# S5 output products issued in pairs of state groups, and a stacked 64-token arm for experts with 129 to 192 tokens

## The chip, the cores and the metric

The kernel runs on one core of one Trainium2 chip, written for the core's own engines: TensorE (PE in the profile, with PEld for its weight loads), VectorE (DVE), ScalarE (ACT), GpSimd (POOL) and SyncE (SP, which issues most loads). The metric is the time of one execution on the device in microseconds (us), lower is better.

## The reference

The reference runs two blocks of two layers each on 512 tokens of width 1024, all in float32. The change lies in the second layer of the first block: an S5 mixer, and a mixture of experts (MoE).

```python
# S5: 64 groups of 16 channels with 64 complex states each, chunks of 64 tokens
bu = jnp.einsum('gpc,btgc->btgp', b_bar, u_c)            # input into the states
...
hs = hs + a_pow[None] * h[:, None]                       # states, carried from chunk to chunk
y = jnp.einsum('gcp,btgp->btgc', c, hs).real             # states to outputs
...
# MoE: each token goes to the 2 of 8 experts with the largest router logits
logits = xt @ w_router + b_router
top_v, top_i = lax.top_k(logits, 2)
gates = softmax(top_v)
y = sum_e gate[:, e] * ((silu(xt @ w1[e]) * (xt @ w3[e])) @ w2[e])    # 1024 -> 1408 -> 1024
```

The inputs are fixed by a seed. Computed from them by the reference's own formulas, the experts get 104, 105, 94, 110, 126, 176, 170 and 139 tokens: three of the eight have more than 128, and all three lie between 129 and 192.

## The kernel before

**Products in three parts.** Large matrices are split into a high part (`hi`, L76, a ScalarE copy to the type fp32r) and a low part (`lo`, L79, VectorE: source minus high part). A product is then three fp32r products, summed in one PSUM bank: high by high, high by low, low by high (`mm3`, L113 to 115, and `mm3s`, L120 to 122, where the weights are the moving operand of 512 columns and 128 tokens stand still in TensorE).

**S5.** The work goes through four batches B of 16 state groups. `front(B)` brings the inputs into U, forms the chunks' input sums (pS, L1018) and on VectorE the states at the start of each 8-token piece (Hs, real and imaginary part; L784 to 789 and the scan L1026, with the table Tab). `back(B)` then forms the outputs in two halves of four pairs q of state groups. For each group m of a pair it issues three plain float32 products on a quarter or half of the array: U by Tt (L1045, 128 rows, 64 columns at column 64m), and Hs[0] by Ca and Hs[1] by Ca (L1048, 64 rows and 64 columns at row and column 64m), all into the half bank p[64m:64m+64]. ScalarE takes the bank out (L1051), it is transposed (pYt, L1057), and VectorE and ScalarE finish it. While back(B) is on TensorE, projections of the next batch, the next front and the following GLU's products (pglu) are issued around it. A load of a batch's tables is queued on SP (L971 ff., L981).

**MoE.** The eight experts are taken one after the other (e = 0 to 7) in an order that the kernel sets from their counts; the three with two blocks come at e = 1, 4 and 7, where the trace has their products; `expert(e, blocks, ...)` is compiled for one block of 128 tokens, `(0,)`, and for two, `(0, 1)`, and a branch on the expert's count, read on each engine (L1607), chooses:

```python
with tc.If(n_e > 128) as two:
    expert(e, (0, 1), XG[e % 2], main, start, nxt, first, then, extra)
with two.Else():
    expert(e, (0,), XG[e % 2], main, start, nxt, first, then, extra)
```

In an expert, tokens are gathered by indirect DMA (`fetch`) and transposed into xg, high and low part (`turn`: pxg, L1456). Six chunks cc of the hidden width follow, 512 columns (256 of w1 and 256 of w3) in five and 256 in the sixth: for each of 8 k and each block, `mm3s` into ph; then silu (L1505, ScalarE), the product with the w3 half (hb, L1507, VectorE), and in `flush` the transposition of hb (phT, L1475) with its split into hT. At last come 11 k with two banks py of 512 columns, and copies of py to y (L1538 on ScalarE, L1539 on VectorE), which a DMA stores. The last expert keeps its output on chip: py is split into high and low parts (`own_y`) for the combining products pyo (L1640). The weights for the first four k of an expert's chunk 0 (`pre`) are split ahead of it, in the expert before; the others come through a ring of loaded units, each split by ScalarE and VectorE when its turn comes.

Of the kernel before, what the change touches and what calls it, by code (L numbers as in the profile page):

```python
# [21 lines left out]
D = 1024  # L22
# [26 lines left out]
class Core:  # L49
# [905 lines left out]
    def s5(self):  # L955
# [3 lines left out]
        with ExitStack() as ctx:  # L959
# [75 lines left out]
            def back(B, U, Hs):  # L1035
                Yn = b2.tile([128, 8, 8, 16], FT, tag="Yn", name="Yn", bufs=1)
                for hf in range(2):
                    Tt, Ca = load_out(B, hf)
                    p = self.bank("bk", "pY")
                    for qq in range(4):  # L1040
                        q = 4 * hf + qq
                        for m in range(2):
                            o = p[64 * m:64 * m + 64, 128 * qq:128 * qq + 128]
                            ks = slice(64 * m, 64 * m + 64)
                            mm(o, U[:, q, m], Tt[:, 2 * qq + m], start=True, stop=False,  # L1045
                               tile_position=(0, 64 * m))
                            for i in range(2):
                                mm(o, Hs[i][ks, q, 0:64],  # L1048
                                   Ca[ks, i, qq, 1:9].rearrange("p t c -> p (t c)"),
                                   start=False, stop=(i == 1), tile_position=(64 * m, 64 * m))  # L1050
# [124 lines left out]
    def _moe(self, m1, m2):  # L1175
# [271 lines left out]
                xs.append(x)  # L1447
            return xs

        def turn(xs, xt, b0=0):  # L1450
            for b, x in enumerate(xs, b0):
                for hf in range(2):
                    p = self.bank("pc", "pxg")
                    for k in range(4):
                        kk = 4 * hf + k
                        nc.tensor.transpose(p[:, k * 128:(k + 1) * 128], x[:, kk * 128:(kk + 1) * 128], ident)  # L1456
                    ks = slice(4 * hf, 4 * hf + 4)
                    q = p.rearrange("p (k n) -> p k n", n=128)
                    self.hi(xt[:, 0, ks, b], q)
                    self.lo(xt[:, 1, ks, b], q, xt[:, 0, ks, b])  # L1460

        def expert(e, blocks, xt, weights, start=None, nxt=None, first=(), then=None, extra=None):
# [3 lines left out]
            hT = {b: [m1.tile([128, 11, 128], FR, tag=f"hT{t}{b % 2}", name="hT") for t in "hl"] for b in blocks}  # L1466
            hb = {}

            def flush(cc, tag="pp"):
                nk = 2 if cc < 5 else 1  # L1470
                p = self.bank(tag, "phT")
                for bi, b in enumerate(blocks):
                    for j in range(nk):
                        c = (bi * nk + j) * 128
                        nc.tensor.transpose(p[:, c:c + 128], hb[cc, b][:, j * 128:(j + 1) * 128], ident)  # L1475
                for bi, b in enumerate(blocks):
                    q = p[:, bi * nk * 128:(bi + 1) * nk * 128]
                    th, tl = (t[:, 2 * cc:2 * cc + nk].rearrange("p k n -> p (k n)") for t in hT[b])
                    self.hi(th, q)
                    self.lo(tl, q, th)  # L1480

            for cc in range(6):
                n = 512 if cc < 5 else 256
                if extra and cc == 0:
                    extra()
                    got = start()
                ps = {b: self.bank("pc", "ph") for b in blocks}

                def product(w, u, b):
                    for k in range(4):  # L1490
                        kk = 4 * u + k
                        self.mm3s(ps[b][:, :n], xt[:, 0, kk, b % 2], xt[:, 1, kk, b % 2], w[0][:, k],
                                  w[1][:, k], start=(kk == 0), stop=(kk == 7))

                for u in range(2):
                    ahead = first and cc == u == 0
                    w = first if ahead else weights.take(pin=bool(mine) and cc == 1, fine=bool(first) and cc == 0)
                    for b in blocks:
                        if ahead and b and mine:
                            turn(mine, xt, 1)  # L1500
                        product(w, u, b)
                h2 = n // 2
                for b in blocks:
                    s = m2.tile([128, 256], FT, tag="sl", name="sl")
                    nc.scalar.activation(s[:, :h2], ps[b][:, :h2], AF.Silu)  # L1505
                    hb[cc, b] = m2.tile([128, 256], FT, tag="hb", name="hb", bufs=4)
                    v.tensor_tensor(hb[cc, b][:, :h2], s[:, :h2], ps[b][:, h2:n], op=OP.mult)  # L1507
                if cc:
                    flush(cc - 1)
            py = {}  # L1510
# [2 lines left out]
            for u in range(6):  # L1513
                w = weights.take(late=u == 5 and then is not None)
                for k in range(2 if u < 5 else 1):
                    kk = 2 * u + k
                    for b in blocks:
                        for j in range(2):
# [10 lines left out]
            for b in blocks:  # L1529
                if e == NE - 1 and not over:  # L1530
                    yh, yl = own_y(b)
                    for j in range(2):
                        c = slice(512 * j, 512 * j + 512)
                        self.hi(yh[:, c], py[b][j])
                        self.lo(yl[:, c], py[b][j], yh[:, c])
                    continue
                y = m2.tile([128, D], FT, tag="y", name="y")
                nc.scalar.activation(y[:, :512], py[b][0], AF.Copy)  # L1538
                v.tensor_copy(y[:, 512:], py[b][1])  # L1539
                if over:  # L1540
                    nc.scalar.dma_start(self.yo_d[128 * (b - 2):128 * (b - 1), :], y)
                else:
                    o = 128 * place(e, b)
                    nc.scalar.dma_start(self.y_d[o:o + 128, :], y)

        def own_y(b):

# [25 lines left out]
        for e in range(NE):  # L1573
# [36 lines left out]
                    which(k)  # L1610
            at, known = main.taken, dict(regs)
            extra = (lists, gates, None)[min(e, 2)]
            with tc.If(n_e > 128) as two:
                expert(e, (0, 1), XG[e % 2], main, start, nxt, first, then, extra)
            main.taken = at
            regs.clear()
            regs.update(known)
            with two.Else():
                expert(e, (0,), XG[e % 2], main, start, nxt, first, then, extra)
            regs.clear()  # L1620
            regs.update(known)

# [664 lines left out]
```

## Time and profile before

| what | value |
|---|---|
| time, median of 3 runs | 2566.69 us (2561.83 to 2568.28) |
| the profiled execution's own time | 2555.23 us |
| its span, first to last instruction | 2553.5 us |
| mean granted TensorE clock, share of full speed | 0.966 |
| TensorE busy | 2397.8 us, 94% of the span |
| VectorE busy | 1692.6 us, 66% |
| ScalarE busy | 1184.1 us, 46% |
| GpSimd busy | 489.7 us, 19% |
| DMA, mean over the span | 147 GB/s |

The busy times overlap, since the engines work side by side. TensorE's is summed over its whole span, and its matmuls run into each other like links of a chain: the time from one row's start to the next row's start says how long a product holds up the next, and the length in the row is longer than that. A row of the form "a<-b,c" writes tile a from tiles b and c, and 128x512 is its size, partitions by elements; on a TensorE row 64*64 or 128*128 is the part of the array (rows by columns) that it uses. In brackets stands the idle time before the row, and what ended it; "issue" means that no tile and no DMA did.

### The profile page before, as it was taken

The page shows a single profiled execution, that of the slowest core. Times are in us where ns is not written, and L with a number is a line of the kernel's source. Part 1 is how long each engine was busy: PE and PEld are TensorE (multiplying, and loading weights), DVE is VectorE, ACT ScalarE, POOL GpSimd, SP SyncE. Part 2 cuts the span into 40 slices and gives each one's busy share as a digit, 9 for nine tenths or more (in the row PEclk, how much of TensorE's full clock was granted, in tenths as well). Part 3 has the DMA queues.
Part 4 walks back from the last instruction along what each step waited for, and adds up shares of the span by engine and source line. Part 5 has one row for each costly group of instructions (what it writes and reads, how often), then busy time and mean ns, then how long its engine had stood idle before and what let it go on. Part 6 is the DMA issues. An engine that isn't in the chain of part 4 may idle for free. (4 is left out here: it accounts for less than half of the span.)

```text
span 2553.5 us, 35019 instructions
## 1 busy us (share of the span) xinstructions
PE 2397.8 (94%) x12769; PEld 1954.3 (77%) x12769; DVE 1692.6 (66%) x3554; ACT 1184.1 (46%) x2133; POOL 489.7 (19%) x585
## 2 busy tenths in 40 slices
PE   8999998979999999988988989999999998999997
PEld 7899987867788867766866777878776778787676
DVE  5877758868845663366567567666787557578466
ACT  5545434322433323245466456545656444556453
POOL 1010123676666101031000000110002013001103
PEclk9999999989999999979999999999999999999998
DMA  4323223556645552356578568834122222223111
GB/s 160 111 78 95 62 83 120 204 164 236 241 144 208 176 146 75 109 178 258 202 259 320 196 231 335 317 108 138 56 89 88 79 91 87 84 75 108 58 50 67
DMA packets 107744, 375.80 MB, mean 147 GB/s; under 512 B 23202, under 2 KB 49218, under 8 KB 77576
## 3 DMA queue, kind: packets, MB, share of 16 engines
q1 hardware_dynamic: 73440, 285.86, 32.4%
q0 software_dynamic: 13552, 61.18, 7.0%
q10 hardware_dynamic: 20536, 26.01, 2.9%
q8 instruction: 120, 1.97, 0.3%
q14 instruction: 96, 0.79, 0.1%
HBM read 335.76 MB, written 37.24 MB: 146 GB/s over the span
## 5 line engine op out<-in xcount | busy, mean ns | idle before, releaser
L79 DVE TENSOR_TENSOR wl<-raw,wh 128x1024 fp32r<-128x1024 f32 (+4 forms) x248 | 295.4, 1194 | 209.7 <-ACT wh L76 205.4
L79 DVE TENSOR_TENSOR wl<-ring,wh 128x1024 fp32r<-128x1024 f32 (+1 forms) x280 | 299.3, 1099 | 116.2 <-ACT wh L76 111.8
L76 ACT ACTIVATE wh<-raw 128x1024 fp32r<-128x1024 f32 (+5 forms) x262 | 246.0, 947 | 275.9 <-PE pp L114 85.8
L113 PE MATMUL pp<-xh,wh 128*128 128x512 f32 (+1 forms) x944 | 348.8, 375 | 4.4 <-ACT wh L76 1.1
L114 PE MATMUL pp<-xl,wh 128*128 128x512 f32 (+1 forms) x944 | 349.2, 370 | 3.2 <-DVE xl L79 3.1
L115 PE MATMUL pp<-xh,wl 128*128 128x512 f32 (+1 forms) x944 | 346.8, 369 | 0.0
L76 ACT ACTIVATE wh<-ring 128x1024 fp32r<-128x1024 f32 (+1 forms) x280 | 257.3, 956 | 123.4 <-PE ph L122 76.0
L113 PEld LDWEIGHTS pp<-xh,wh 128*128 128x128 f32 x944 | 179.9, 193 | 38.2 <-issue 3.7
L114 PEld LDWEIGHTS pp<-xl,wh 128*128 128x128 f32 x944 | 181.4, 192 | 32.0 <-DVE xl L79 4.0
L115 PEld LDWEIGHTS pp<-xh,wl 128*128 128x128 f32 x944 | 181.1, 192 | 28.2 <-issue 1.8
L121 PE MATMUL ph<-wl,xg 128*128 128x512 f32 (+1 forms) x484 | 181.5, 376 | 1.1 <-DVE wl L79 1.1
L122 PE MATMUL ph<-wh,xg 128*128 128x512 f32 (+1 forms) x484 | 180.6, 375 | 0.0
L120 PE MATMUL ph<-wh,xg 128*128 128x512 f32 (+1 forms) x484 | 179.3, 381 | 0.1
L115 PE MATMUL pf<-xh,wl 128*128 128x512 f32 (+1 forms) x384 | 145.4, 379 | 3.9 <-DVE wl L79 3.9
L114 PE MATMUL pf<-xl,wh 128*128 128x512 f32 (+1 forms) x384 | 145.8, 381 | 0.0
L113 PE MATMUL pf<-xh,wh 128*128 128x512 f32 (+1 forms) x384 | 145.3, 380 | 0.5 <-ACT xh L76 0.5
L121 PEld LDWEIGHTS ph<-wl,xg 128*128 128x128 f32 x484 | 91.2, 188 | 20.6 <-DVE wl L79 2.9
L122 PEld LDWEIGHTS ph<-wh,xg 128*128 128x128 f32 x484 | 91.0, 188 | 17.7
L1739 DVE SCALAR_TENSOR_TENSOR adaacc<-adaraw,sc,adaacc 128x512 f32<-128x512 f32 x84 | 92.5, 1101 | 17.9 <-DMA adaraw<-w_ada 16.8
L120 PEld LDWEIGHTS ph<-wh,xg 128*128 128x128 f32 x484 | 89.7, 189 | 16.8 <-ACT wh L76 0.6
L121 PE MATMUL py<-wl,hT 128*128 128x512 f32 x242 | 97.7, 404 | 4.1 <-DVE wl L79 4.1
L122 PE MATMUL py<-wh,hT 128*128 128x512 f32 x242 | 95.6, 397 | 0.0
(707 smaller groups left out, 5509.6 us busy)
## 6 DMA issues: line engine op xcount, KB each, us to landing
ring<-moe SPq DMA_DIRECT2D x120, 1024.0 KB, 6.2
raw<-w_in SPq DMA_DIRECT2D x30, 1024.0 KB, 4.9
adaraw<-w_ada POOLq DMA_DIRECT2D x24, 1024.0 KB, 5.4
raw<-w SPq DMA_DIRECT2D x22, 1024.0 KB, 5.7
ring<-moe SPq DMA_DIRECT2D x24, 512.0 KB, 5.5
raw<-w SPq DMA_DIRECT2D x16, 704.0 KB, 4.2
raw<-w_glu SPq DMA_DIRECT2D x8, 1024.0 KB, 5.1
raw<-w_out SPq DMA_DIRECT2D x8, 1024.0 KB, 4.8
```

Source lines behind the costliest of these rows:

```text
L76: return self.nc.scalar.activation(dst, src, AF.Copy, **kw)
L79: return (eng or self.nc.vector).tensor_tensor(dst, src, hi.bitcast(FT), op=OP.subtract)
L113: mm(ps, wh, xh, start=start, stop=False)
L114: mm(ps, wh, xl, start=False, stop=False)
L115: return mm(ps, wl, xh, start=False, stop=stop)
L120: mm(ps, ah, wh, start=start, stop=False)
L121: mm(ps, ah, wl, start=False, stop=False)
L122: return mm(ps, al, wh, start=False, stop=stop)
L1739: v.scalar_tensor_tensor(acc, r[:, k], s, acc, op0=OP.mult, op1=OP.add)
```

## The change

There are two parts, which don't touch each other.

In the S5 `back`, the products of the two groups m of a pair are taken in turn: both U by Tt products first, then both products with Hs[0], then both with Hs[1]. Number, sizes and places of the products stay as they were.

In the MoE, an expert with more than 128 tokens gets one of two arms: with more than 192, the two full blocks as before; with 129 to 192, an arm in which the second block has 64 tokens. Their high parts stand in columns 0 to 63 of one tile and the low parts in columns 64 to 127, so that for each k one product of 128 columns by the weights' high part forms high by high in PSUM rows 0 to 63 and low by high in rows 64 to 127, and one of 64 columns by the weights' low part adds high by low to rows 0 to 63 (`stacked`). `fold` adds the two halves of the bank: a ScalarE copy of rows 64 to 127 to SBUF and a VectorE addition. It is done once for each chunk ahead of silu and twice for each py.

```diff
@@ s5, back @@
+o = [p[64 * m:64 * m + 64, 128 * qq:128 * qq + 128] for m in range(2)]
 for m in range(2):
-    o = p[64 * m:64 * m + 64, 128 * qq:128 * qq + 128]
-    ks = slice(64 * m, 64 * m + 64)
-    mm(o, U[:, q, m], Tt[:, 2 * qq + m], start=True, stop=False, tile_position=(0, 64 * m))
-    for i in range(2):
-        mm(o, Hs[i][ks, q, 0:64], Ca[ks, i, qq, 1:9]..., start=False, stop=(i == 1), tile_position=(64 * m, 64 * m))
+    mm(o[m], U[:, q, m], Tt[:, 2 * qq + m], start=True, stop=False, tile_position=(0, 64 * m))
+for i in range(2):
+    for m in range(2):
+        ks = slice(64 * m, 64 * m + 64)
+        mm(o[m], Hs[i][ks, q, 0:64], Ca[ks, i, qq, 1:9]..., start=False, stop=(i == 1), tile_position=(64 * m, 64 * m))
@@ moe, expert @@
+def stacked(p, x, wh, wl, first, last):
+    if first:
+        mm(p, x, wh, start=True, stop=False)
+    last_ = mm(p[:64], x[:, :64], wl, start=False, stop=False)
+    return last_ if first else mm(p, x, wh, start=False, stop=last)
+def fold(dst, p):
+    nc.scalar.activation(dst, p[64:128], AF.Copy)
+    v.tensor_tensor(dst, p[0:64], dst, op=OP.add)
...
 def product(w, u, b):
+    if b == half:
+        for k in range(4):
+            kk = 4 * u + k
+            stacked(ps[b][:, :n], xt[:, 0, kk, b], w[0][:, k], w[1][:, k], kk == 0, kk == 7)
+        return
...
 for b in blocks:
+    r, p = rows[b], ps[b]
+    if b == half:
+        p = folds[:64, cc % 2]
+        fold(p[:, :n], ps[b][:, :n])
     s = m2.tile([128, 256], FT, tag="sl", name="sl")
-    nc.scalar.activation(s[:, :h2], ps[b][:, :h2], AF.Silu)
+    nc.scalar.activation(s[:r, :h2], p[:r, :h2], AF.Silu)
...
 for b in blocks:
+    r, p = rows[b], py[b]
+    if b == half:
+        y = folds... if e == NE - 1 else m2.tile([128, D], FT, tag="y", name="y")
+        p = [y[:64, 512 * j:512 * j + 512] for j in range(2)]
+        for j in range(2):
+            fold(p[j], py[b][j])
...
@@ moe, the loop over experts @@
 with tc.If(n_e > 128) as two:
-    expert(e, (0, 1), XG[e % 2], main, start, nxt, first, then, extra)
+    with tc.If(n_e > 192) as full:
+        arm((0, 1))
+    with full.Else():
+        arm((0, 1), 1)
 with two.Else():
-    expert(e, (0,), XG[e % 2], main, start, nxt, first, then, extra)
+    arm((0,))
```

`arm` sets the state of the weight stream back and calls `expert` with the block that is half. The transpositions of the half block (`turn`, `flush`) take 64 rows in place of 128, and the parts are written to the two column halves of one tile.

In the first of the last batch's output pairs, TensorE's rows before read as follows. Hs_8791 and Hs_8792 are the real and imaginary states, and 64x128 is the part of the bank that is written.

```order
L1045 MATMUL pY<-Tt,U 64x128
L1048 MATMUL pY<-Ca,Hs_8791 64x128
L1048 MATMUL pY<-Ca,Hs_8792 64x128
L1045 MATMUL pY<-Tt,U 64x128
L1048 MATMUL pY<-Ca,Hs_8791 64x128
L1048 MATMUL pY<-Ca,Hs_8792 64x128
```

In the changed kernel the same place reads:

```order
L1045 MATMUL pY<-Tt,U 64x128 x2
L1049 MATMUL pY<-Ca,Hs_8791 64x128 x2
L1049 MATMUL pY<-Ca,Hs_8792 64x128 x2
L1045 MATMUL pY<-Tt,U 64x128 x2
L1049 MATMUL pY<-Ca,Hs_8791 64x128 x2
```

The six products of a pair now stand as three pairs of one kind, with the two groups m side by side; the work ahead of the batch and behind it stands where it stood.

At the entry into the fifth expert (e = 4), TensorE's rows before are these: the end of the arm before, the read of the count, the branch, and the first products.

```order
L122 MATMUL py<-wh,hT 128x512
L1613 UNCONDITIONAL_BRANCH
L1607 TENSOR_LOAD cnti
L1613 COMPARE_AND_BRANCH
L120 MATMUL ph<-pre,xg 128x512
L121 MATMUL ph<-pre,xg 128x512
```

In the changed kernel there:

```order
L122 MATMUL py<-wh,hT 128x512
L1670 UNCONDITIONAL_BRANCH
L1657 TENSOR_LOAD cnti
L1670 COMPARE_AND_BRANCH
L1671 COMPARE_AND_BRANCH
L120 MATMUL ph<-pre,xg 128x512
```

A second branch stands behind the first; what follows it in the order is the arm of two full blocks, and the arm of the half block lies behind that one, so that an expert with 129 to 192 tokens reaches it by a jump.

The end of the half block's chunk 0 in the same expert reads before (as a full block):

```order
L120 MATMUL ph<-wh,xg 128x512
L121 MATMUL ph<-wl,xg 128x512
L122 MATMUL ph<-wh,xg 128x512
L120 MATMUL ph<-wh,xg 128x512
L121 MATMUL ph<-wl,xg 128x512
L122 MATMUL ph<-wh,xg 128x512
L1475 MATMUL phT<-cst,hb 128x128 x2
```

and in the changed kernel's half arm:

```order
L1483 MATMUL ph<-wl,xg 64x512
L1484 MATMUL ph<-wh,xg 128x512
L1483 MATMUL ph<-wl,xg 64x512
L1484 MATMUL ph<-wh,xg 128x512
L1498 MATMUL phT<-cst,hb 128x64 x2
```

Two products stand for each k where there were three, and a product of 64 columns lies between each two of 128; the transposition of block 1's hb stands directly behind them, as it did.

## Rows read from the trace of the kernel before

**Rows 1.** Busy time by engine in three stretches: S5, expert 4, expert 5.

```profile
core 0: us, PE busy (x) PEld busy (x) DVE busy (x) ACT busy (x) POOL busy (x), PEclk, DMA share, GB/s
872.00:972.60 100.60, 99.47 (x814) 71.97 (x814) 56.64 (x84) 21.14 (x34) 0.45 (x4) 1.00 0.45 132
1401.40:1501.30 99.90, 98.30 (x459) 78.87 (x457) 52.38 (x67) 45.24 (x68) 0.94 (x1) 1.00 0.59 217
1507.80:1558.90 51.10, 50.44 (x229) 40.28 (x229) 44.12 (x51) 37.46 (x51) 3.72 (x2) 0.97 0.81 299
```

**Rows 2.** Groups of S5's products: count, busy us, mean ns, idle before.

```profile
L1048 PE MATMUL pY<-Ca,Hs 64*64 64x128 f32 x256 | 40.8, 282 | 0.0
L1045 PE MATMUL pY<-Tt,U 128*64 128x128 f32 x128 | 27.3, 296 | 0.4 <-issue 0.4
```

**Rows 3.** TensorE in S5 by time: start, us, engine, line, records.

```profile
894.28 0.43 PE L1045 MATMUL pY<-Tt,U 128*64 128x128 f32 x2
894.64 0.65 PE L1048 MATMUL pY<-Ca,Hs 64*64 64x128 f32 x4
895.22 0.43 PE L1045 MATMUL pY<-Tt,U 128*64 128x128 f32 x2
895.58 0.66 PE L1048 MATMUL pY<-Ca,Hs 64*64 64x128 f32 x8
896.17 0.43 PE L1045 MATMUL pY<-Tt,U 128*64 128x128 f32 x2
...
913.52 2.08 PE L1018 MATMUL pS<-U,Gt 128*64 128x64 f32 x64
```

**Rows 4.** The last batch's states on VectorE, and SP's issue of its table.

```profile
938.00 0.69 DVE L785 TENSOR_TENSOR s5v<-pS,Tab 128x512 f32<-128x512 f32 x1 [5.15 <-PE pS L1018]
...
946.85 0.69 DVE L789 TENSOR_TENSOR Hs<-Hs,s5v 128x512 f32<-128x512 f32 x1
...
927.39 0.38 SPq L971 DMA_DIRECT2D Tab<-s_tab  x1
```

**Rows 5.** Groups of the experts' products over the whole span.

```profile
L121 PE MATMUL ph<-wl,xg 128*128 128x512 f32 x396 | 156.9, 397 | 1.1 <-DVE wl L79 1.1
L121 PE MATMUL py<-wl,hT 128*128 128x512 f32 x242 | 97.7, 404 | 4.1 <-DVE wl L79 4.1
```

**Rows 6.** TensorE's first products of expert 4 by time.

```profile
1401.36 0.39 PE L120 MATMUL ph<-pre,xg 128*128 128x512 f32 x1
1401.59 0.39 PE L121 MATMUL ph<-pre,xg 128*128 128x512 f32 x1
```

**Rows 7.** TensorE at 1814 us: products on all and on half the rows.

```profile
1814.84 0.50 PE L1865 MATMUL pix<-ik,iq 128*128 128x512 f32 x1
1815.27 0.50 PE L1866 MATMUL pix<-ik,iq 64*128 64x512 f32 x1
1815.70 0.50 PE L113 MATMUL pp<-xh,wh 128*128 128x512 f32 x1
1816.04 0.40 PE L114 MATMUL pp<-xl,wh 128*128 128x512 f32 x1
```

**Rows 8.** The 11 branches of L1613 (ns, min/median/max), then expert 3's entry.

```profile
L1613 PEldq COMPARE_BRANCH  x11: 70/4501/6034, 1113.4 to 1707.5; - x11
...
1349.03 0.77 PE L120 MATMUL ph<-pre,xg 128*128 128x512 f32 x1 [5.30 <-issue]
...
1349.00:1353.00 4.00, 3.97 (x9) 3.17 (x10) 2.28 (x2) 0.83 (x1) 0.00 (x0) 0.50 1.01 407
```

**Rows 9.** TensorE's waits in expert 1.

```profile
1186.28 0.89 PE L1456 MATMUL pxg<-cst,xgn 128*128 128x128 f32 x4 [3.10 <-DVE hotT L1434]
...
1195.21 0.44 PE L1475 MATMUL phT<-cst,hb 128*128 128x128 f32 x2 [0.93 <-DVE hb L1507]
```

**Rows 10.** Copies of py out of PSUM at expert 4's end.

```profile
1499.25 0.60 ACT L1538 ACTIVATE y<-py 128x512 f32<-128x512 f32 x1 [8.04 <-PE py L122]
...
1499.95 0.69 DVE L1539 COPY y<-py 128x512 f32<-128x512 f32 x1 [7.48 <-PE py L122]
```

More of the change, by code (lines that the diff above doesn't have):

```diff
@@ L1041, in back @@
                         q = 4 * hf + qq
+                        o = [p[64 * m:64 * m + 64, 128 * qq:128 * qq + 128] for m in range(2)]
                         for m in range(2):
-                            o = p[64 * m:64 * m + 64, 128 * qq:128 * qq + 128]
-                            ks = slice(64 * m, 64 * m + 64)
-                            mm(o, U[:, q, m], Tt[:, 2 * qq + m], start=True, stop=False,
-                               tile_position=(0, 64 * m))
-                            for i in range(2):
-                                mm(o, Hs[i][ks, q, 0:64],
-                                   Ca[ks, i, qq, 1:9].rearrange("p t c -> p (t c)"),
+                            mm(o[m], U[:, q, m], Tt[:, 2 * qq + m], start=True, stop=False, tile_position=(0, 64 * m))
+                        for i in range(2):
+                            for m in range(2):
+                                ks = slice(64 * m, 64 * m + 64)
+                                mm(o[m], Hs[i][ks, q, 0:64], Ca[ks, i, qq, 1:9].rearrange("p t c -> p (t c)"),
                                    start=False, stop=(i == 1), tile_position=(64 * m, 64 * m))
@@ L1448, in fetch, with turn @@
             return xs
-        def turn(xs, xt, b0=0):
+        def turn(xs, xt, b0=0, rows=128):
             for b, x in enumerate(xs, b0):
@@ L1455, in turn, with expert @@
                         kk = 4 * hf + k
-                        nc.tensor.transpose(p[:, k * 128:(k + 1) * 128], x[:, kk * 128:(kk + 1) * 128], ident)
+                        nc.tensor.transpose(p[:, k * 128:k * 128 + rows], x[:rows, kk * 128:(kk + 1) * 128], ident[:rows, :rows])
                     ks = slice(4 * hf, 4 * hf + 4)
[L1458 to L1462, printed above, removed]
+                    q = p.rearrange("p (k n) -> p k n", n=128)[:, :, :rows]
+                    th, tl = (xt[:, 0, ks, b, c:c + 64] for c in (0, 64)) if rows == 64 else (xt[:, a, ks, b] for a in range(2))
+                    self.hi(th, q)
+                    self.lo(tl, q, th)
+        def expert(e, blocks, xt, weights, start=None, nxt=None, first=(), then=None, extra=None, half=None):
             over = blocks[0] > 1
@@ L1465, in expert @@
             got = start() if start and not extra else None
-            hT = {b: [m1.tile([128, 11, 128], FR, tag=f"hT{t}{b % 2}", name="hT") for t in "hl"] for b in blocks}
+            hT = {b: [m1.tile([128, 11, 128], FR, tag=f"hT{t}{b % 2}", name="hT") for t in "hl"[:1 + (b != half)]] for b in blocks}
             hb = {}
+            if half and not mine:
+                v.tensor_copy(xt[:, 0, :, half, 64:128], xt[:, 1, :, half, 0:64])
+            if half:
+                folds = m1.tile([128, 2, 512], FT, tag="hTl1", name="folds")
+            rows = {b: 64 if b == half else 128 for b in blocks}
+            def stacked(p, x, wh, wl, first, last):
[6 more added lines that the diff above has]
+                v.tensor_tensor(dst, p[0:64], dst, op=OP.add)
             def flush(cc, tag="pp"):
@@ L1472, in flush @@
                 for bi, b in enumerate(blocks):
+                    r = rows[b]
                     for j in range(nk):
                         c = (bi * nk + j) * 128
-                        nc.tensor.transpose(p[:, c:c + 128], hb[cc, b][:, j * 128:(j + 1) * 128], ident)
+                        nc.tensor.transpose(p[:, c:c + r], hb[cc, b][:r, j * 128:(j + 1) * 128], ident[:r, :r])
                 for bi, b in enumerate(blocks):
                     q = p[:, bi * nk * 128:(bi + 1) * nk * 128]
+                    if b == half:
+                        q = q.rearrange("p (k n) -> p k n", n=128)[:, :, :64]
+                        th, tl = (hT[b][0][:, 2 * cc:2 * cc + nk, c:c + 64] for c in (0, 64))
+                        self.hi(th, q)
+                        self.lo(tl, q, th)
+                        continue
                     th, tl = (t[:, 2 * cc:2 * cc + nk].rearrange("p k n -> p (k n)") for t in hT[b])
@@ L1499, in expert @@
                         if ahead and b and mine:
-                            turn(mine, xt, 1)
+                            turn(mine, xt, 1, rows[1])
                         product(w, u, b)
@@ L1503, in expert @@
                 for b in blocks:
+                    r, p = rows[b], ps[b]
+                    if b == half:
+                        p = folds[:64, cc % 2]
+                        fold(p[:, :n], ps[b][:, :n])
                     s = m2.tile([128, 256], FT, tag="sl", name="sl")
-                    nc.scalar.activation(s[:, :h2], ps[b][:, :h2], AF.Silu)
+                    nc.scalar.activation(s[:r, :h2], p[:r, :h2], AF.Silu)
                     hb[cc, b] = m2.tile([128, 256], FT, tag="hb", name="hb", bufs=4)
-                    v.tensor_tensor(hb[cc, b][:, :h2], s[:, :h2], ps[b][:, h2:n], op=OP.mult)
+                    v.tensor_tensor(hb[cc, b][:r, :h2], s[:r, :h2], p[:r, h2:n], op=OP.mult)
                 if cc:
@@ L1517, in expert @@
                     for b in blocks:
+                        if b == half:
+                            for j in range(2):
+                                c = slice(512 * j, 512 * j + 512)
+                                last = stacked(py[b][j], hT[b][0][:, kk], w[0][:, k, c], w[1][:, k, c], kk == 0, kk == 10)
+                            continue
                         for j in range(2):
@@ L1529, in expert @@
             for b in blocks:
+                r, p = rows[b], py[b]
+                if b == half:
+                    y = folds.rearrange("p a n -> p (a n)") if e == NE - 1 else m2.tile([128, D], FT, tag="y", name="y")
+                    p = [y[:64, 512 * j:512 * j + 512] for j in range(2)]
+                    for j in range(2):
+                        fold(p[j], py[b][j])
                 if e == NE - 1 and not over:
@@ L1533, in expert @@
                         c = slice(512 * j, 512 * j + 512)
-                        self.hi(yh[:, c], py[b][j])
-                        self.lo(yl[:, c], py[b][j], yh[:, c])
+                        self.hi(yh[:r, c], p[j])
+                        self.lo(yl[:r, c], p[j], yh[:r, c])
                     continue
-                y = m2.tile([128, D], FT, tag="y", name="y")
-                nc.scalar.activation(y[:, :512], py[b][0], AF.Copy)
-                v.tensor_copy(y[:, 512:], py[b][1])
+                if b != half:
+                    y = m2.tile([128, D], FT, tag="y", name="y")
+                    nc.scalar.activation(y[:, :512], py[b][0], AF.Copy)
+                    v.tensor_copy(y[:, 512:], py[b][1])
                 if over:
@@ L1543, in expert @@
                     o = 128 * place(e, b)
-                    nc.scalar.dma_start(self.y_d[o:o + 128, :], y)
+                    nc.scalar.dma_start(self.y_d[o:o + r, :], y[:r])
         def own_y(b):
@@ L1612, in _moe, with arm @@
             extra = (lists, gates, None)[min(e, 2)]
+            def arm(blocks, half=None):
+                main.taken = at
+                regs.clear()
+                regs.update(known)
+                expert(e, blocks, XG[e % 2], main, start, nxt, first, then, extra, half)
             with tc.If(n_e > 128) as two:
-                expert(e, (0, 1), XG[e % 2], main, start, nxt, first, then, extra)
-            main.taken = at
-            regs.clear()
-            regs.update(known)
+                with tc.If(n_e > 192) as full:
+                    arm((0, 1))
+                with full.Else():
+                    arm((0, 1), 1)
             with two.Else():
-                expert(e, (0,), XG[e % 2], main, start, nxt, first, then, extra)
+                arm((0,))
             regs.clear()
```

## The prediction

> **What bounds it now.** I looked first at the page's busy shares: TensorE is at 94% and no other engine is above 66%, so the time is mostly a row of products, and a change is worth what it takes out of that row. Whether this also holds in the two stages that change, the busy times by stretch tell [rows 1]. In S5 TensorE is busy for 99.5 of 100.6 us, and in expert 4, which has two blocks, for 98.3 of 99.9, with VectorE at 52.4, ScalarE at 45.2 and the DMA engines at 0.59 of their time. Expert 5, with one block, takes 51.1 us, and there the DMA share is 0.81: the weights are the same, the time is half. So in the stages with two blocks neither loads nor splits are the limit, and both parts act on an engine that has nothing else to wait for. The spacing of products by time gives their prices, and the waits and branches what stands between them.
>
> **S5 as it is.** A float32 product has two records. For one group m of a pair, two records of U by Tt and four with Hs follow each other [rows 2 and 3]: from 894.28 to 894.64 is .36 us, to 895.22 another .58, so .94 for a group and, for the 64 groups (128 records over 2, or 256 over 4), some 60 us of the stretch's 100.6. The 64 short products of pS, which alternate between two column halves of the array, take little more than their 2.08 us together, .03 each [rows 3]: products on different parts of the array run side by side. The row of eight Hs records at 895.58 shows the same for the quarter tiles (0, 0) and (64, 64): from there to 896.17 is .59 us, what four alone take. These eight write two banks.
>
> **S5 changed.** The order puts the two groups' products in turn, so that a pair q should take one .36 and one .58 to .60, about .96 where it took 1.88. For 32 pairs this is 30.7. Before, 64 by .94 are 60.2, and I take 59.6, since in the row of eight a few already overlap: a gain of 28.9. Not all of it arrives: the last batch's Hs comes from a chain of 12 VectorE operations that runs from 938.00 to 947.54 beside products [rows 4], with TensorE having less left to cover it, and its table is issued at 927.39, 10.6 us ahead of its use. I take 2 us off, a choice between nothing and the 5.15 us that VectorE itself waited for pS: **27**. Bounds: where the tiles of one bank take turns, only the fixed part of each change of kind is saved. Of the .36 and .58, .14 each does not grow with the records (two more records cost .22), two such per pair are saved, and the Tt pairs still overlap by .22: .50 by 32 = 16, less late loads 15. Above stands 28.9.
>
> [...]
>
> **The experts.** 396 products ph of 512 columns with wl are 36 for each of 11 blocks, and 242 py are 22 [rows 5]: eight blocks and three second ones. By the counts all three second blocks have 129 to 192 tokens, so each goes to the new arm. It has two products for each k where there were three: 40 (ph), 8 (ph of 256 columns) and 22 (py, 11 k by two banks) fall away. The spacing is .23 (1401.36 to 1401.59) [rows 6]; 62 by .232 and 8 by .12 are **15.4 us an expert**. The time of a product goes by its 512 moving columns, and these stay, so that I give the ones of 64 tokens the same .23. No row has such a product: as the lower bound I see the same .23, the upper one is that of D below.
>
> Put in are these:
> - *Folds.* Eight for each expert, .60 on ScalarE and .69 on VectorE each [rows 10]: 4.8 and 5.5 us, into 54.7 and 47.5 idle us of these engines [rows 1]. Behind chunks 1 to 5 the next chunk's products stand ahead of the transposition that wants hb. Chunk 0's does not have that cover: phT stands directly behind block 1's products in the order, and waits .93 for hb already [rows 9]. There the fold adds 1.3, in e1 and e4. Without cover in all chunks it would be 6 by 1.3 = 7.8 an expert.
> - *The tail of e7.* pyo follows the split of py at once. Two folds go ahead of it, .60 + .69 and one more .69 with some overlap, and VectorE has xn to finish: 2.5.
> - *The jump.* The branch has 11 runs on TensorE, of .07 us at the least and 4.5 in the middle [rows 8]. The .07 are those where the arm follows: expert 4 goes on with its first product at .23 [rows 6]. [...] In the new order the two full blocks stand behind the branches and the half arm behind these, so that e1, e4 and e7, which paid nothing, now pay **7.1 each**. In e1 3.1 of it replace a wait for hotT [rows 9]. Bounds: nothing, if the instructions were at hand, and 9.
> - *Weights.* Waits for wl are 5.2 us in all [rows 5]. With a stage shorter by a tenth some more come up: 2 an expert, between 0 and the 5.
>
> e1: 15.4 − 1.3 − 7.1 + 3.1 − 2 = 8.1. e4: 15.4 − 1.3 − 7.1 − 2 = 5.0. e7: 15.4 − 2.5 − 7.1 − 2 = 3.8. Together **17**. The other experts take the same way as before, one taken branch to the arm of one block.
>
> [...]
>
> **The sum.** 27 + 17 = 44. The profiled execution took 2555.2, so 2511. It lies 11.5 under the median of 2566.7 that the result will stand beside; on that the same 44 make **2523**. About 0.3%, 7.7 us, is what a measurement of this kernel can tell from no change.
>
> **The rivals.**
> - *B, S5's quarter tiles take turns.* 15 for S5 and 17 for the experts: 32, 2535. For it: the overlap seen was between two banks. Against it: pS alternates in one bank, though by column halves. Chance .14.
> - *C, the second blocks give nothing.* If the folds delay every chunk, 7.8 an expert in place of 1.3 and of nothing, most of the 17 are gone: 27 remain, 2540. For it: the bank of a chunk now comes free later, after the fold. Against: half of both engines' time is idle. Chance .10.
> - *E, the jump is cheap or covered.* The experts give 38 (17 and three by 7.1), in all 64: 2503. Against: all taken branches in the trace cost. Chance .05.
> - *D, the other side: TensorE empties itself at each change between 128 and 64 columns.* Of an expert's 70 products of 64 columns, 64 lie alone between two of 128. Where TensorE goes between all rows and 64 rows, the spacing is .43, .43 and .34 in place of .23 [rows 7], so .50 for going there and back. 64 by .50 are 32 an expert, 96 in all, and 96 − 44 = 52 us slower: 2619. It decides from 44 over 192 changes, .23 each. For it: the .14 for a change of kind in S5. Against it: rows 7 change the rows, not the columns, and in the compiled program of the changed kernel the new fp32r products name all four column groups of the array as their neighbours do, where S5's 64-column ones name two. Chance .11.
>
> [...]
>
> **How the numbers follow.** The forecast has .58, B .14, C .10, E .05, D .11, and .02 that neither part pays. Its own range is 2512 to 2533: S5 by 24 to 29, the experts by 10 to 26. With B and C the range reaches to 2544; below, a cheaper jump leads to 2506. E's end and D are left out. Faster by over 0.3%: .58 + .14 + .10 + .05 = .87. D at half price is no change: .03 of it, with the .02, is .05 for the same, and .08 remain for slower.
>
> **What would show it.** In S5, pairs of Tt and Hs products with some .96 from pair to pair, and the stretch of 100.6 us some 27 shorter; Hs products at 1.2 a pair would be B. In e1, e4 and e7, gaps of 5 us ahead of the first product with the clock at .50 behind; products of 64 columns spaced .23, where .4 or more would be D; phT's wait at chunk 0 near 2.2; and expert 4's stretch at 95 in place of 99.9. Waits of phT in every chunk would be C. It would be wrong above all if the new products have a spacing that no row of before shows.

## The result, and the profile after

The changed kernel takes 2533.66 us (median of 4 runs, 2530.74 to 2536.57); the kernel before took 2567.49 beside it. The ratio is 0.9872, 95% interval 0.9852 to 0.9892, so it is faster by 33 us (28 to 38). The forecast was 2523 and a gain of 44. The direction held and the time lies within the wide range of 2506 to 2544, but 0.7 us outside the forecast's own, 2512 to 2533; a quarter of the gain didn't come.

The profiled execution after has a span of 2534.8 us. The busy times in the same three stretches as in [rows 1], S5, expert 4 and expert 5 of the changed kernel, read:

```profile
874.30:955.30 81.00, 74.03 (x814) 55.36 (x814) 56.32 (x84) 21.20 (x34) 0.45 (x4) 0.96 0.61 164
1386.30:1477.20 90.90, 87.17 (x388) 65.18 (x388) 50.65 (x68) 44.82 (x69) 0.95 (x1) 0.96 0.56 208
1484.50:1536.90 52.40, 51.25 (x229) 40.96 (x229) 44.13 (x51) 37.91 (x52) 1.94 (x2) 0.95 0.80 295
```

S5's stretch, with the same 814 records of TensorE, is shorter by 19.6 us. TensorE was busy for all but 1.1 us of it and now stands idle for 7.0, at a clock of 0.96. Expert 4 lost 9 us, but the stretch begins behind its jump; with the gap of 6.5 ahead of it, it is 97, where 95 was forecast.

In S5 TensorE's rows by time show what [rows 3] promised:

```profile
895.87 0.44 PE L1045 MATMUL pY<-Tt,U 128*64 128x128 f32 x4
896.24 0.65 PE L1049 MATMUL pY<-Ca,Hs 64*64 64x128 f32 x8
896.83 0.44 PE L1045 MATMUL pY<-Tt,U 128*64 128x128 f32 x4
```

From pair to pair it is .96 us, and the eight Hs records of one bank take .59, what four took before. Quarter tiles that write one bank do run side by side here, in disjoint rows of the bank.

Of the experts, these are expert 4's products at the end of the half block's chunk 0, by time:

```profile
1398.60 0.39 PE L1484 MATMUL ph<-wh,xg 128*128 128x512 f32 x1
1398.82 0.40 PE L1483 MATMUL ph<-wl,xg 128*64 128x512 f32 x1
1399.06 0.40 PE L1484 MATMUL ph<-wh,xg 128*128 128x512 f32 x1
1401.83 0.34 PE L1498 MATMUL phT<-cst,hb 64*128 64x64 f32 x2 [2.37 <-DVE hb L1545]
```

The product of 64 columns is spaced .22 to .24 from its neighbours, as in [rows 6], and the wait at phT is 2.37 where it was .93 [rows 9]: both as forecast. At the entries the rows answering to [rows 8] are these (the branches of the second `If` in ns, three entries and three exits, then expert 4's first product, expert 7's, and the windows behind expert 7's entry):

```profile
L1671 PEldq COMPARE_BRANCH  x6: 3443/5988/6546, 1160.6 to 1684.0; - x6
...
1386.29 0.77 PE L120 MATMUL ph<-pre,xg 128*128 128x512 f32 x1 [6.06 <-issue]
...
1600.28 0.77 PE L120 MATMUL ph<-pre,xg 128*128 128x512 f32 x1 [5.47 <-issue]
...
1600.30:1604.40 4.10, 2.09 (x5) 1.51 (x6) 2.08 (x2) 0.64 (x1) 0.19 (x1) 0.50 1.03 422
1604.40:1609.00 4.60, 4.60 (x12) 3.32 (x12) 0.00 (x0) 0.00 (x0) 3.58 (x4) 0.50 0.95 385
```

The gaps of 5 us and more stand at two of the three entries where they were expected; expert 1's has none (.7 in the table below). The clock behind expert 7's stays at .50 for nearly 9 us, with a wait of 2 us in it.

The table takes the starts of TensorE's products from four traces: two of the kernel before, the changed one, and one that the experiments come to. S5 is from the first pu to the last pglu, an expert from its first ph to its last py, a gap from the last py to the next ph, the tail from the last py to the first pxo.

| us | before | before, again | changed | half arm first |
|---|---|---|---|---|
| S5 | 247.3 | 249.6 | 230.0 | 229.3 |
| expert 0 (not changed) | 56.9 | 66.7 | 61.9 | 62.2 |
| gap ahead of 1 | 0.4 | 0.3 | 0.7 | 0.4 |
| expert 1 | 104.3 | 104.3 | 93.9 | 94.5 |
| gap behind it | 9.9 | 10.1 | 12.9 | 13.1 |
| gap ahead of 4 | 0.2 | 0.2 | 6.5 | 0.2 |
| expert 4 | 99.6 | 99.6 | 90.7 | 88.8 |
| gap behind it | 6.8 | 7.5 | 7.5 | 8.5 |
| gap ahead of 7 | 0.2 | 0.2 | 5.9 | 0.2 |
| expert 7 | 94.7 | 94.6 | 86.5 | 81.2 |
| tail | 15.3 | 15.3 | 18.6 | 18.4 |

### The profile page after: what moved, and what is told of

It is laid out like the page before. It is cut to its first block, busy times and chain, and to the rows that moved or that the text cites. A ratio compares the mean times of both kernels' runs of the same rounds, so it can differ in the third digit from the quotient of the medians.

```text
span 2534.8 us, 34641 instructions
## 1 busy us (share of the span) xinstructions
PE 2343.4 (92%) x12559; PEld 1900.2 (75%) x12559; DVE 1699.7 (67%) x3577; ACT 1194.0 (47%) x2155; POOL 493.9 (19%) x585
## 4 chain that ended last, share of the span: by engine, by line
PE 41%; DVE 4%; issue 2%; ACT 2%; DMA 1%; ACTq 0%; DVEq 0%
PE pp L113 6%; PE pp L114 6%; PE pp L115 6%; PE ph L120 3%; PE ph L121 2%; PE ph L122 2%; PE pv L1875 2%; PE ptp L1863 1%; DMA ring<-moe 1%; PE psc L2118 1%; PE psc L1923 1%; DVE wl L79 1%; PE pn L120 1%; PE pn L121 1%; PE ph L1483 1%
## 5 line engine op out<-in xcount | busy, mean ns | idle before, releaser
L121 PE MATMUL ph<-wl,xg 128*128 128x512 f32 (+1 forms) x352 | 134.1, 381 | 1.0 <-DVE wl L79 1.0
L122 PE MATMUL ph<-wh,xg 128*128 128x512 f32 (+1 forms) x352 | 132.3, 376 | 0.0
L120 PE MATMUL ph<-wh,xg 128*128 128x512 f32 (+1 forms) x352 | 131.9, 386 | 0.3 <-ACT wh L76 0.3
L1445 POOL DMA_INDIRECT xgn<-xn_d,lst x10 | 16.2, 1618 | 373.7 <-PE pxg L1457 170.5
L1858 ACT ACTIVATE s<-s,sst 128x128 f32<-128x128 f32 (+3 forms) x128 | 71.1, 557 | 36.0 <-DVE sst L1856 34.3
L115 PEld LDWEIGHTS pf<-xh,wl 128*128 128x128 f32 x384 | 74.6, 195 | 16.8 <-DVE wl L79 4.3
L1866 ACT ACTIVATE PT<-ptp 128x128 f32<-128x128 f32 (+3 forms) x128 | 51.9, 434 | 71.1 <-PE ptp L1863 56.2
L114 PEld LDWEIGHTS pf<-xl,wh 128*128 128x128 f32 x384 | 74.6, 194 | 14.3 <-DVE xl L79 1.6
```

Source lines behind the costliest of these rows:

```text
L114: mm(ps, wh, xl, start=False, stop=False)
L115: return mm(ps, wl, xh, start=False, stop=stop)
L120: mm(ps, ah, wh, start=start, stop=False)
L121: mm(ps, ah, wl, start=False, stop=False)
L122: return mm(ps, al, wh, start=False, stop=stop)
L1858: nc.scalar.activation(s, s, AF.Exp, scale=-1.0, bias=st[:, 0:1], accum_out=st[:, 1:2])
```

## The experiments

All times stand beside runs of the kernel before of the same job (medians 2564.9 to 2567.7).

| kernel | median us | ratio to before, 95% interval |
|---|---|---|
| S5 part alone (s5_only) | 2543.89 | 0.9911, 0.9885 to 0.9936 |
| experts' part alone (moe_only) | 2559.38 | 0.9973, 0.9957 to 0.9990 |
| half arm first (half_first) | 2520.15 | 0.9818, 0.9797 to 0.9840 |
| Tab on GpSimd's queue (tab_pool) | 2533.99 | 0.9882, 0.9861 to 0.9903 |
| half of Ca not loaded (less_ca) | 2527.01 | 0.9852, 0.9826 to 0.9878 |
| half arm first, xn earlier (hf_tail) | 2523.64 | 0.9835, 0.9809 to 0.9861 |
| half arm first, Tab on GpSimd (hf_tab) | 2516.50 | 0.9799, 0.9770 to 0.9828 |
| half arm only (half_only) | 2519.33 | 0.9816, 0.9790 to 0.9842 |
| stores beside the last jump (dma_jump) | 2551.23 | 0.9934, 0.9911 to 0.9957 |
| half arm first, later phT (hf_late) | 2516.59 | 0.9809, 0.9792 to 0.9827 |
| half first, Tab, later phT (best) | 2518.09 | 0.9803, 0.9783 to 0.9823 |

**The two parts apart.** Each kernel has one hunk of the diff and the other part as before.

> The S5 part alone, with the experts of the kernel before. The prediction's own term is 27 us, so about 2540. The theory from the changed kernel's trace is that the pairs do save 29 but that the last batch's table now arrives 5 us after its sums and TensorE waits and then runs at the lower clock, so that 17 to 20 remain: about 2549. If the quarter tiles took turns in a bank it would be 15.

> The experts' part alone, with the S5 of the kernel before. The prediction's term is 17 us: about 2550. The rival, read off the one profiled execution of the changed kernel, is that entries, tails and waits eat nearly all of it and 3 to 6 us remain: about 2562. The two parts alone should add up to the 34 us that both together gave.

S5 alone gives 23 us (16 to 30), the experts alone 7 (3 to 11); with 33 for both, that adds up within the intervals. The larger miss is the experts': 7 for 17.

**The order of the arms.**

```diff
 with tc.If(n_e > 128) as two:
-    with tc.If(n_e > 192) as full:
-        arm((0, 1))
-    with full.Else():
-        arm((0, 1), 1)
+    with tc.If(n_e <= 192) as part:
+        arm((0, 1), 1)
+    with part.Else():
+        arm((0, 1))
```

> The changed kernel with the arm of the half block placed directly behind the two branches, and the arm of two full blocks behind that. If a jump into the half arm costs 7.1 us at each of three entries, of which 3.1 replace another wait, this is 15 to 18 us faster than the changed kernel: about 2517, and the first products of experts 4 and 7 follow without a gap of 5 us. If the gap comes from anything else (the weights, the gathered tokens), it stays and the time is that of the changed kernel, 2534.

Against the changed kernel's 0.9872 the ratio 0.9818 is 14 us more, and the intervals lie apart. TensorE's rows at expert 4's entry in this kernel:

```profile
1385.88 0.40 PE L122 MATMUL py<-wh,hT 128*128 128x512 f32 x1
1386.12 0.39 PE L120 MATMUL ph<-pre,xg 128*128 128x512 f32 x1
```

The gap is gone (.24), at expert 7's too. So it was the jump. By the table it cost 6.3 and 1.9 of slow products at expert 4, 5.7 and 5.3 at expert 7, and at expert 1 next to nothing: .7 against .4. There TensorE's sequencer, which takes the branches, came to the branch (1160.58 to 1164.17) just as a wait of 9.2 us for gathered tokens ended, with a queue of products still to run at a clock of .50, and they covered it.

**The table of S5, and the transfers.** The theory was that the last batch's table Tab comes late.

```diff
-nc.sync.dma_start(Tab, self.s5_tab[B])
+nc.gpsimd.dma_start(Tab, self.s5_tab[B])
```

> The changed kernel with the table Tab of S5 loaded by GpSimd's queue in place of SP's, where it stands behind the loads of Tt. If the last batch's chain waits for this table, it starts some 5 us earlier, right behind its sums pS, the wait of 3.3 us at the last outputs and the lower clock behind it go, and the time is 5 to 8 us less: about 2527. If the wait is set by the transfers' total, the table comes earlier and Tt later, and nothing is gained: 2534.

```diff
-Ca = b1.tile([128, 2, 4, 9, 16], FT, tag="Ca", name="Ca", bufs=3)
-nc.sync.dma_start(Ca, self.s5_ca[2 * B + i])
+if i == 0:
+    self.s5_cur = b1.tile([128, 2, 4, 9, 16], FT, tag="Ca", name="Ca", bufs=3)
+    nc.sync.dma_start(self.s5_cur, self.s5_ca[2 * B])
+Ca = self.s5_cur
```

> The changed kernel with half of the loads of Ca left out: the second half of each S5 batch uses the Ca of the first half, so its output is not the reference's. 2.3 MB less are loaded in the 80 us of S5. If S5's lost gain is due to the transfers' total there (DMA share 0.8 to 1.15 from 890 to 930 us), the waits at the last batch (0.8 and 3.3 us) and the low clock behind them shrink and S5 takes 5 to 8 us less: S5's stretch some 223 in place of 230, the time about 2527. If the late table is a matter of its queue or of its buffer alone, S5 stays at 230 and the time at 2534.

The changed kernel's rows (SP's issue of Tab, VectorE's first step on the last batch, TensorE's first outputs of it, and the clock behind them):

```profile
922.51 0.38 SPq L971 DMA_DIRECT2D Tab<-s_tab  x1
...
930.20 0.69 DVE L785 TENSOR_TENSOR s5v<-pS,Tab 128x512 f32<-128x512 f32 x1 [7.58 <-PE pY L1049]
...
940.90 0.70 PE L1045 MATMUL pY<-Tt,U 128*64 128x128 f32 x4 [3.28 <-issue]
...
940.90:946.50 5.60, 5.60 (x40) 3.33 (x40) 3.32 (x5) 2.19 (x4) 0.00 (x0) 0.50 0.00 0
```

In [rows 4] the step at 938.00 followed its sums at once. Here the last sum pS starts at 924.7 and the step at 930.20; the releaser named, pY, had long been done, so it is the table. With Tab on GpSimd's queue:

```profile
918.15 0.54 POOL L971 DMA_DIRECT2D Tab<-s_tab  x1 [4.13 <-DVE Hs L787]
...
928.43 0.69 DVE L785 TENSOR_TENSOR s5v<-pS,Tab 128x512 f32<-128x512 f32 x1 [4.78 <-DMA Tab<-s_tab]
...
939.13 0.44 PE L1045 MATMUL pY<-Tt,U 128*64 128x128 f32 x4 [0.89 <-issue]
```

It is issued 4.4 us earlier and used 1.8 earlier: 10.3 us from issue to use, where SP's took 7.7. The outputs follow the table: in both traces they start 1.17 us behind the end of the last step on Hs (939.73 and 937.96). In this one trace S5 takes 223.4 in place of 230.0. From the first output to the last it is 68.5 us, and 70.7 and 70.5 in the two later kernels with the table on GpSimd's queue (hf_tab, best); the seven traces of the new order with the table on SP's queue have 71.0 to 74.4, the three of the old order 93.4. So the queue is worth some 3 us in the traces, less than the times resolve: 2533.99. The windows from 910 and 920 us, before, changed, and with half of Ca left out, tell why an earlier issue is worth no more:

```profile
910.00:920.00 10.00, 10.00 (x118) 7.05 (x116) 4.73 (x8) 0.60 (x1) 0.00 (x0) 1.00 0.69 228
920.00:930.00 10.00, 9.99 (x66) 7.62 (x65) 6.90 (x12) 1.82 (x4) 0.22 (x2) 1.00 0.87 213
```

```profile
910.00:920.00 10.00, 9.09 (x84) 7.09 (x82) 10.00 (x17) 2.04 (x4) 0.23 (x2) 1.00 0.99 300
920.00:930.00 10.00, 9.19 (x153) 6.27 (x148) 2.49 (x5) 2.41 (x5) 0.00 (x0) 1.00 1.15 229
```

```profile
910.00:920.00 10.00, 9.09 (x84) 7.11 (x82) 10.00 (x16) 1.87 (x4) 0.23 (x2) 1.00 0.92 220
920.00:930.00 10.00, 10.00 (x162) 6.97 (x160) 6.81 (x13) 3.05 (x6) 0.00 (x0) 1.00 0.59 153
```

The DMA engines (the last share, which counts a packet's whole time where it starts and so can pass 1) went from 0.69 and 0.87 to 0.99 and 1.15: the same bytes in a shorter stage. With fewer bytes TensorE has no gap from 920 to 930, and the table's rows are these:

```profile
921.52 0.38 SPq L971 DMA_DIRECT2D Tab<-s_tab  x1
...
926.31 0.69 DVE L785 TENSOR_TENSOR s5v<-pS,Tab 128x512 f32<-128x512 f32 x1 [3.06 <-DMA Tab<-s_tab]
```

It is issued by the same queue, 1.0 us earlier, and used 4.8 us after its issue in place of 7.7. From the first output to the last it is 66.8 us where the changed kernel has 73.9, and S5 takes 220.2, 27 and 29 us under the two traces of before, about as much as the pairs save. By the ratios the time is 5 us under the changed kernel's, but the two intervals overlap, so the traces carry this and not the time. Of the 9 us that S5's stretch lacks, 7 lie in the transfers; two waits of .67 and .91 for U stay here too.

**What else stands in the experts.**

```diff
+if nxt and e == NE - 1 and cc == 3:
+    nxt(got)
...
-if nxt and u == (4 if e == 0 else 2):
+if nxt and e < NE - 1 and u == (4 if e == 0 else 2):
```

The edit stands on half_first, as the next kernel's does.

> The kernel with the half arm first, and in it the eight additions to xn on VectorE of the last expert made from its fourth chunk on in place of its output products. If the folds of the last expert's tail are late because VectorE still works on xn, the stretch from the last py to pxo goes from 18.4 to about 16.5 us; the time is then 2518. If the chain of fold, high part and low part itself is the price, it stays 18.4.

> The kernel with the half arm first, and the S5 table loaded by GpSimd's queue. If the two are worth what their traces show, 14 us and 3 to 6, the time is 2515; if the table's queue moves the wait only, 2520.

The tail goes from 18.4 to 17.8 us, so some .6 of its 3 us is xn; the rest is put down to the chain of fold, high and low part, which no run takes apart. The time doesn't show it. With the table on GpSimd's queue the time is 3.7 under half_first's, within the intervals.

```diff
 with tc.If(n_e > 128) as two:
-    with tc.If(n_e > 192) as full:
-        arm((0, 1))
-    with full.Else():
-        arm((0, 1), 1)
+    arm((0, 1), 1)
```

> The changed kernel without the second branch and without the arm of two full blocks, so that it would not serve an expert with more than 192 tokens (these inputs have none). Entry into the half arm as with the half arm first, without a gap. At the end of the half arms of experts 1 and 4 TensorE's jump took 6.0 and 6.2 us in the changed kernel, 3.4 and 4.9 before; if it is longer because of the arm in the middle, the gaps behind these experts go back from 12.9 and 7.5 to about 10 and 7 us and the time is 2516; if the length of a jump does not depend on what lies between, 2520 as with the half arm first.

The time is that of half_first, and the gaps behind experts 1 and 4 stay at 12.5 and 7.6. The arm in the middle isn't the reason that they grew.

```diff
+if e == NE - 1 and not over and u == 2:
+    late = hT[0][0].rearrange("p k n -> p (k n)").bitcast(FT)
+    for i in range(8):
+        nc.sync.dma_start(self.s5_g[i].rearrange("p a b c -> p (a b c)"), late[:, 384:])
+    ...   # the same into s5_tab (4) and s5_ca (8)
```

> The changed kernel with 10 MB of stores that nobody needs, from a finished tile to dead scratch memory, put on SP's queue in the last expert's output products. In the traces a taken branch on TensorE took 3.4 to 3.6 us where the DMA engines were at 0.3 or less of their time, 4.3 to 4.9 at 0.3 to 0.6, and 5.8 to 8.6 at 0.7 to 1.0. The jump at the last expert's end took 3.45 at a share of 0.02. If a jump waits for a transfer among the other transfers, it now takes 6 or more with a share of 0.7 or more, and ends behind the last product. If the length goes with the place in the program, it stays at 3.4 to 3.6.

The windows below are cut to one jump of TensorE each: at expert 1's end before; there after; at expert 7's end after; and at that same end with the added stores, with the branch's own row and the first product behind it.

```profile
1276.53:1279.90 3.37, 3.37 (x16) 2.73 (x15) 0.40 (x1) 0.60 (x1) 0.00 (x0) 1.00 0.28 109
```

```profile
1254.43:1260.45 6.02, 4.34 (x19) 2.96 (x17) 2.06 (x3) 1.78 (x3) 0.00 (x0) 1.00 0.74 300
1684.01:1687.46 3.45, 3.19 (x14) 2.09 (x12) 3.31 (x4) 1.59 (x4) 0.00 (x0) 1.00 0.02 5
```

```profile
1689.09:1695.55 6.46, 3.18 (x14) 2.08 (x12) 6.32 (x8) 3.09 (x6) 0.00 (x0) 0.97 1.02 401
...
L1679 PEldq COMPARE_BRANCH  x6: 3295/6252/6463, 1165.5 to 1689.1; - x6
...
1695.72 1.62 PE L1705 MATMUL pyo<-xg,hotT 128*128 128x512 f32 x3 [3.45 <-issue]
```

The same jump at the same place takes 3.45 us at a DMA share of 0.02 and 6.46 at 1.02. The DMA's packets show what falls into it. These are lines of the DMA view: for the jump in the changed kernel (1684 to 1687.5 us), then with the added stores for the jump's first 4 us (1689 to 1693) and for the rest (1693 to 1695.6):

```profile
DMA packets 1, 0.02 MB, mean 5 GB/s; under 512 B 0, under 2 KB 0, under 8 KB 0
q8 instruction: 1, 0.02, 2.0%
...
q1 hardware_dynamic: 438, 1.60, 101.8%
...
q1 hardware_dynamic: 283, 1.03, 100.5%
q8 instruction: 1, 0.02, 2.3%
```

One packet of instructions, 16 KB, falls into the jump. By the packet records of the traces it starts 1.0 us into the jump in the changed kernel and 4.1 with the stores; it takes 1.1 and 1.0, and the jump ends 1.3 behind it both times. So the added length lies ahead of the packet's start. With that the grown gap behind expert 1 has its reason: the half arm ends sooner, the next weights are still on their way (0.74 against 0.28), the packet starts 3.5 us into the jump in place of 1.0, and the jump takes 6.0 in place of 3.4 and outlasts the products that covered it.

This one, too, stands on half_first; `product` gives back its last product.

```diff
-product(w, u, b)
+done = product(w, u, b)
+if u == 0 and b == blocks[0]:
+    mark = done
...
-    flush(cc - 1)
+    with tc.issue_after(mark.ins) if cc == 1 and half else nullcontext():
+        flush(cc - 1)
```

> The kernel with the half arm first, and the transposition of chunk 0's hb in a half arm issued behind the first block's first four k of chunk 1 in place of directly behind chunk 0. In experts 1 and 4 TensorE waited 2.4 us there, and 3 us of products at the lower clock followed. If this wait and this clock are the price of the fold, each of the two experts takes some 3 us less: expert 4 some 86 in place of 88.8, expert 1 some 91.5 in place of 94.5, in all about 2514. If the products then wait for the split weights in its place, the experts stay where they are and the time is 2520.

TensorE's longest waits in expert 4 of this kernel (in total, times, longest):

```profile
PE ph L120 <- ACT wh L76: 2.9, 1, 2.9
PE ph L1482 <- DVE xg L79: 0.7, 1, 0.7
```

The wait for hb is gone and one for the split weights of 2.9 us stands in its place; expert 4 takes 89.3. The rival was right in that a wait of about the same length comes up for ScalarE's split. That ScalarE does the fold, silu and the splits one after the other, and whichever TensorE asks for first is late, is a reading of this row; no run takes the splits off it.

> All three together: the half arm first, the table of S5 on GpSimd's queue, and the later transposition. If they add up, 2516.5 less 6: about 2510. If the later transposition is worth nothing, 2516.

They don't add up further: half_first, hf_tab, half_only, hf_late and this one lie from 2516.5 to 2520.2 with intervals that overlap. What can be said is that the half arm first is worth 14 us over the changed kernel, and that the other two edits are worth nothing that these times resolve.

> The kernel before once more, for a second trace. Its first trace took 56.9 us for expert 0, and those of five other kernels, one of them with the same experts, took 61.4 to 64.6. If that first one is an exception, this one shows 61 or more there, and a difference of 5 us between the traces before and after at expert 0 is no effect of the change.

Expert 0 took 66.7 us in the second trace, the execution 2575.1; in the thirteen traces other than the first it lies between 61.0 and 66.7. The 56.9 of the trace that the prediction read was an exception, so the 5 us that expert 0 seems to have lost are no effect of the change.

## Why the prediction was right, and where its sizes were off

The forecast's mechanism came about, and its direction. That the time lies in the stated range is owed, by 0.7 us and so within the noise, to the part of it that was added for the rivals B and C, and neither of these came about.

- **The mechanism of both parts held.** Pairs of state groups at .96, 64-column products at .23, a full stop of TensorE at two of three entries, phT at 2.4 (forecast 2.2). Rival D, the emptying at each change of 64 and 128 columns, is out: 70 products an expert show no price. In the changed kernel's trace the 167 of 64 columns and 512 moving ones that run at the full clock without a wait start .23 to .24 ahead of the next product.
- **B is out as a mechanism, and its number came near all the same.** The eight Hs records of one bank run in .59, where four took .58, so no wait for the bank shows, at least between these tiles, which write disjoint partitions.
- **S5's late end was mis-sized: 2 us taken off, 9 measured.** 28.9 less 2 made 27; the stretch is shorter by 19.6. The last outputs waited 3.28 (.43 before), smaller waits of .91, .81, .68 and .67 came up, three pairs at the lower clock took 5.03 in place of 2.9, and the pair behind them .4 more than its .96. That is 8.4; the last .9 is not placed. The time of s5_only, 23 less, can't tell 20 from 27. The term that failed: I looked at the queue's issue of the table and not at the DMA share of the stage once it is shorter. The chain on VectorE that waits for the table has 14 operations, two of them scans, and not 12.
- **The jumps' sum was right, its parts not.** 7.1 at each entry less 3.1 made 18.2. The 7.1 was an estimate from the one entry into expert 3 [rows 8], 5.30 without a product and then nine products in 3.97 at a clock of .50, where nine by .232 are 2.1; no run shows it at the entries that changed. There by the table it is 8.2 at expert 4, 11.0 at expert 7 and .3 at expert 1, together 19.5; half_first gave 14 in time and 15 in the traces. Expert 1's hidden jump made up for expert 7's long stay at the lower clock. The 3.1 that I took off for hotT had nothing to do with it: that wait is still there, 2.9 us.
- **The exits were not in the sum at all.** I left the end of an arm as it was. It costs 2.9 us behind expert 1; the .4 behind expert 4 is less than the two traces of before differ by.
- **Smaller terms.** The tail cost 3.3 for 2.5. Chunk 0's wait cost 1.4 (forecast 1.3), but in experts 1 and 4 it also brings the clock down (0.80 over the 4 us behind it): with the half arm first these two gained 9.8 and 10.8, and expert 7, which has no such wait, 13.5.

The experts' sum by the table is 8.6: expert 1 gives 10.4 less .3 at its entry and 2.9 at its exit, expert 4 gives 8.9 less 6.3 and .4, expert 7 gives 8.2 less 5.7 and 3.3. In time it was 7, and 17 was forecast. Rivals C and E did not come about: only chunk 0 has the wait, and the jumps are not cheap, though E's "covered" is what expert 1's was. The trace before had covered ones too, against what I held against E: the window at 1276.53 above has TensorE busy for all of its 3.37 us. And E's 38 keeps the 3.1 of hotT, though without a jump nothing replaces that wait; it is 35. That the total of 33 lies beside B's 32 is chance.

## What to carry to other kernels

Products of a quarter of the array that go in turn to disjoint parts of a bank ran side by side here (eight records in .59 us, where four took .58), but a stage made a fifth shorter must be asked whether its transfers still fit: look at the DMA share before (0.69 and 0.87 here, which went to 0.99 and 1.15), and scale it. Put the arm that runs directly behind its branch: here a jump to it cost 6 us and the slow clock behind it another 2 to 5. TensorE paid twice for its short waits here: for the 3.28 us ahead of S5's last outputs, and for the 5.6 us at half clock behind them.

## What the runs showed of the hardware

- **The taken branches on TensorE ended behind a packet of instructions, and with the DMA engines at 0.7 of their time and above that packet started later than at 0.02.** In the fourteen traces such branches took 3.3 to 3.7 us at a share of 0.02, 3.3 to 5.6 at 0.27 to 0.63, and 5.5 to 8.7 at 0.7 and above; with 10 MB of stores put beside it one went from 3.45 to 6.46. In each of these 140 there is a 16 KB packet of the queue q8, "instruction" in the profile: it starts 0.9 to 1.0 us into the jump at a share of 0.02 and 2.7 to 6.3 at 0.7 and above, takes 0.9 to 1.6 in either, and the jump ends 1.3 to 1.6 behind it. The one jump of .4, at the last expert's end in half_only, has no such packet in it.
- **The sequencer ran ahead of the array.** In the changed kernel's trace, where products were queued, a jump began some 4 us ahead of the last product's start (1254.43 against 1258.37) and was covered by them for that long; where the last products had waited for weights, it began with the last one (1594.15 against 1594.40) and stood free.
- **A product on 64 of the array's columns took a full one's time**, .23 for 512 moving columns in fp32r, as one on 128 did: half the columns saved nothing here, only the count of products did.
